# Token mixer of a two-layer network: 64-column chunk matrices, both head pairs in turn, and a scan whose own values are made beforehand

## The chip, the core and the metric

The kernel runs on one core of a Trainium2 chip. The core has a matrix engine (TensorE, PE in the rows; its weight loads are listed apart as PEld), a vector engine (VectorE, DVE), a scalar engine (ScalarE, ACT), GpSimd (POOL), a queue that issues transfers (SyncE, SP) and 16 DMA engines. Each engine works through its own instructions in a fixed order and waits on semaphores for the others. Matmuls read SBUF and write PSUM, which has eight banks of 512 float32 columns for each of 128 partitions. The metric is device time of one execution in microseconds (us).

## The reference

The network is two blocks (feed-forward, token mixer, feed-forward, gated embedding, each closed by a layer norm) and then a second part with attention and experts. Only the token mixer concerns us; it runs twice. Its third of the mixed width called GDN is a gated delta rule in chunks of 64 tokens, for 4 heads of 128:

```python
gcum = jnp.cumsum(g, axis=-1)
decay = jnp.exp(jnp.where(incl, gcum[..., :, None] - gcum[..., None, :], -jnp.inf))
k_beta = k * beta[..., None]
m = jnp.where(strict, jnp.einsum('nbhik,nbhjk->nbhij', k_beta, k) * decay, 0.0)   # 64 x 64 a chunk
t_inv = lax.linalg.triangular_solve(eye + m, jnp.broadcast_to(eye, m.shape), left_side=True, lower=True)
u = jnp.einsum('nbhij,nbhjv->nbhiv', t_inv, v * beta[..., None])
w = jnp.einsum('nbhij,nbhjk->nbhik', t_inv, k_beta * jnp.exp(gcum)[..., None])
qk = jnp.einsum('nbhik,nbhjk->nbhij', q, k) * decay

def step(state, xs):                       # over 4 chunks, one after the other
    u_c, w_c, qk_c, q_c, k_c, gl = xs
    v_new = u_c - jnp.einsum('bhik,bhkv->bhiv', w_c, state)
    o = jnp.einsum('bhik,bhkv->bhiv', q_c, state) + jnp.einsum('bhij,bhjv->bhiv', qk_c, v_new)
    state = state * gl[..., None, None] + jnp.einsum('bhik,bhiv->bhkv', k_c, v_new)
    return state, o
```

The other two thirds are stick-breaking attention (4 heads of 64, 256 tokens, float32) and a gated short convolution. The three results are concatenated and projected.

## The kernel before, in words

All 256 tokens are two tiles of 128 (`NT`). A weight matrix comes from HBM in pieces of 1 MB (`piece`), each split by ScalarE and VectorE into a high and a low part (`split`, lines 303 and 304), and each product with them is three matmuls (`mm3`, and `proj_T` at line 539 for projections that come out transposed, tile `pT`).

`token_mix` (line 935) lays out the work. `gdn_z` and `gdn_ab` project the gate; `gdn_qkv` projects key, query and value of one head pair (two heads) with their convolution; `gdn_gates` and `gdn_rows` make the decay rows. `gdn_prepare` (line 681), called once for each head pair, solves the triangular systems. It puts a tile of 128 tokens, that is two chunks of 64, into one 128 x 128 matrix whose off-diagonal 64 x 64 blocks are zero by the mask. The inverse is built in levels of 4, 16 and 64: helper `mul` (line 707) does four 128 x 128 products for the pair, two in each of two PSUM tiles, and VectorE (`L718`) or ScalarE (`L715`) takes each tile out. Tiles: `U` and `Dm` the masked matrix, `T1`/`T2` the helper product, `X` the inverse, `XT` its transpose, `NT` a product between levels, `wT` the matrix w, `aT` the query-key matrix (it overwrites `g_e`), `kdec` and `qd` decayed key and query, `vb` value times beta.

`gdn_scan` (line 777) goes through four chunks (`t`, `cc`). For each it makes X times values and w times state in one PSUM accumulation (lines 797 and 799), copies it to `vn`, makes the state's increment (line 810), the new state (`L822`, VectorE), and the output (line 831 with the state, line 832 with `vn`). Row and column slices `r` are the chunk's 64 partitions. `stick_breaking` gives four generators, one a head; `weave` advances the scan and at most two heads by turns. `short_conv` comes last.

What sets the order: a scheduler places instructions on each engine by priority, which follows the order of the program text; `later(-1000)` gives a part an earlier priority. Projections (`pT`, `pj`) fill the places between. PSUM tiles come from three pools: `mm_bank` and `ch_bank` with three banks each, `tr_bank` with two. SBUF work tiles come from rings (`s`, `g`, `gc`).

Of the kernel before, what the change touches and what calls it, by code (L numbers as in the profile page):

```python
# [12 lines left out]
ALU = mybir.AluOpType  # L13
AX = mybir.AxisListType
PSUM = bass.MemoryType.PSUM
P = 128

# [34 lines left out]
class Net:  # L52
# [82 lines left out]

    def col(self, n, name, dtype=F32):
        return self.tmp.tile([P, n], dtype, tag=f"col{n}", name=name)

# [12 lines left out]
    def masks(self):  # L151
# [31 lines left out]
        self.m4 = block("m4", self.su, 4)  # L183
        s16 = block("s16", self.su, 16, self.s("s16")[:, :P])
        self.m16 = self.c([P, P], "m16")
        g.tensor_tensor(self.m16, s16, self.m4, ALU.subtract)
        self.m64 = block("m64", self.su, 64)
        g.tensor_tensor(self.m64, self.m64, s16, ALU.subtract)
# [343 lines left out]
    def proj_T(self, src, use):  # L532

        xT = self.xT
        for j, (hi, lo) in enumerate(self.piece(src, KD, 2 * P, by=1)):
            o = self.mm_bank("pT")
# [41 lines left out]
    def gdn_gates(self, i, ab):  # L578
# [42 lines left out]
        rows = [self.gdn_rows(gr, g, beta, gc) for gr in range(2)]  # L621
        return dict(beta=beta, kd=kd, egl=egl, beg=beg, rows=rows)

    def gdn_rows(self, gr, g, beta, gc):
# [8 lines left out]
        eg, e, br = self.g("g_eg"), self.g("g_e"), self.g("g_br")  # L633
        e4 = e.rearrange("p (n w) -> p n w", n=4)
        nc.vector.tensor_tensor(e4, pr.rearrange("p (n w) -> p n w", n=4), self.bl(gc[:, s], P), ALU.subtract)
        nc.vector.tensor_scalar(e, e, 0.0, None, ALU.min)
        self.tact(e, e, AF.Exp)
        nc.vector.tensor_tensor(e4, e4, self.bc(self.mi, 4), ALU.mult)
# [7 lines left out]
        return eg, e, br  # L646
# [15 lines left out]
    def l2n(self, src, out, bias):  # L662
# [4 lines left out]
        pn = self.mm_bank("l2p")  # L667
# [5 lines left out]
    def gdn_qkv(self, i, gr):  # L673
        out = []
        for c0 in (4, 0, 8):
# [5 lines left out]
    def gdn_prepare(self, gr, G, kqv):  # L681
# [4 lines left out]
        eg, E, br = G["rows"][gr]  # L686
        kn, qn, vc = kqv
        n4 = lambda z: z.rearrange("p (n w) -> p n w", n=4)
        self.l2n(kn, kn, 0.0)
        kb, qd = self.g("kb"), self.g("qd")  # L690
        v.tensor_tensor(kb, kn, br, ALU.mult)
        self.l2n(qn, qn, self.c_lns)
        sl = [slice(n * P, n * P + P) for n in range(4)]
        hf = [slice(n * S, n * S + S) for n in range(2)]
        n2 = lambda z: z.rearrange("p (n w) -> p n w", w=P)
        U = self.g("U")
        for j in range(2):
            p = self.ch_bank("pkk")
            for n in (2 * j, 2 * j + 1):
                mm(p[:, sl[n]], kn[:, sl[n]], kb[:, sl[n]], start=True, stop=True)  # L700
            v.tensor_tensor(U[:, hf[j]], p[:, hf[j]], E[:, hf[j]], ALU.mult)
        Dm, T1, L1 = self.g("Dm"), self.g("T1"), self.g("L1")
        for j in range(2):
            v.tensor_tensor(n2(Dm[:, hf[j]]), n2(U[:, hf[j]]), self.bc(self.m4, 2), ALU.mult)
            v.tensor_tensor(n2(T1[:, hf[j]]), self.bc(self.ident, 2), n2(Dm[:, hf[j]]), ALU.subtract)

        def mul(name, l, r, base, o=None):

            o = self.g(name) if o is None else o
            for j in range(2):  # L710
                p = self.ch_bank(name)
                for n in (2 * j, 2 * j + 1):
                    mm(p[:, sl[n]], l[:, sl[n]], r[:, sl[n]], start=True, stop=True)
                if base is None:
                    nc.scalar.activation(o[:, hf[j]], p[:, hf[j]], AF.Copy)  # L715
                else:
                    b = self.bc(self.ident, 2) if base is self.ident else n2(base[:, hf[j]])
                    v.tensor_tensor(n2(o[:, hf[j]]), b, n2(p[:, hf[j]]), ALU.subtract)  # L718
            return o

        DT = self.g("DT")
        for j in range(2):
            p = self.ch_bank("pd")
            for n in (2 * j, 2 * j + 1):
                nc.tensor.transpose(p[:, sl[n]], Dm[:, sl[n]], self.ident)
            nc.scalar.activation(DT[:, hf[j]], p[:, hf[j]], AF.Copy)
        T1 = mul("T2", DT, T1, self.ident, T1)
        v.tensor_tensor(n4(L1), n4(U), self.bc(self.m16, 4), ALU.mult)
        XT = mul("XT", T1, DT, self.ident)
        X = mul("X", DT, T1, self.ident)  # L730
        v.tensor_tensor(n4(U), n4(U), self.bc(self.m64, 4), ALU.mult)
        v.tensor_tensor(qd, qn, eg, ALU.mult)
        aT = E
        for j in range(2):
            p = self.ch_bank("pqk")
            for n in (2 * j, 2 * j + 1):
                mm(p[:, sl[n]], kn[:, sl[n]], qn[:, sl[n]], start=True, stop=True)
            v.tensor_tensor(aT[:, hf[j]], p[:, hf[j]], E[:, hf[j]], ALU.mult)
        for lev, L in enumerate((L1, U)):
            NTm = mul("NT", L, XT, None)  # L740
            T = mul("T1", NTm, X, X)
            if lev == 0:
                cs = slice(gr * 4, gr * 4 + 4)
                col = lambda z: self.bl(z[:, cs], P)
                pk = self.ch_bank("pk")
                for n in range(4):
                    nc.tensor.transpose(pk[:, sl[n]], kn[:, sl[n]], self.ident)
                kg, kdec, vb = self.g("kg"), self.g("kdec"), self.g("vb")
                v.tensor_tensor(n4(kg), n4(pk), col(G["beg"]), ALU.mult)
                v.tensor_tensor(n4(kdec), n4(pk), col(G["kd"]), ALU.mult)  # L750
                pv = self.ch_bank("pv")
                for n in range(4):
                    nc.tensor.transpose(pv[:, sl[n]], vc[:, sl[n]], self.ident)
                v.tensor_tensor(n4(vb), n4(pv), col(G["beta"]), ALU.mult)
# [4 lines left out]
        wT = mul("wT", kg, X, None)  # L759
        return dict(X=X, wT=wT, vb=vb, qd=qd, aT=aT, kdec=kdec)  # L760

# [14 lines left out]

    def gdn_scan(self, G, H, zs, mT):

# [3 lines left out]
        po = [self.tr_bank("gdn_o") for _ in range(NT)]  # L782
        ends = []
        for t in range(NT):
            vn = self.g("vn")
            for cc in range(2):
                r = slice(cc * 64, cc * 64 + 64)
                sl = lambda h: slice((h % 2) * S + t * P, (h % 2) * S + t * P + P)
                sc = lambda h: slice((h % 2) * S + t * P + cc * 64, (h % 2) * S + t * P + cc * 64 + 64)
                last = t == NT - 1 and cc == 1  # L790
                pb = [self.ch_bank("gdn_vS") for _ in range(2)]
                for pr in range(2):
                    A = H[pr]
                    for j in range(2):
                        h = 2 * pr + j
                        hs = slice(j * P, j * P + P)
                        mm(pb[pr][r, hs], A["X"][:, sc(h)], A["vb"][:, sl(h)], start=True, stop=St[pr] is None)
                        if St[pr] is not None:
                            mm(pb[pr][r, hs], A["wT"][:, sc(h)], St[pr][:, hs], start=False, stop=True)
                yield  # L800
                for pr in range(2):
                    nc.vector.tensor_copy(vn[r, pr * S:pr * S + S], pb[pr][r, :S])
                yield
                old = list(St)
                for pr in range(2):
                    if last:
                        continue
                    for j in range(2):
                        h = 2 * pr + j
                        mm(pb[pr][:, S + j * P:S + j * P + P], H[pr]["kdec"][r, sl(h)], vn[r, h * P:h * P + P], start=True, stop=True)  # L810
                yield
                for pr in range(2):
                    if last:
                        continue
                    Sn = self.tmp.tile([P, S], F32, name="gdn_St", bufs=4)
                    if St[pr] is None:
                        nc.vector.tensor_copy(Sn, pb[pr][:, S:])
                    else:
                        for j in range(2):
# [3 lines left out]
                                                           pb[pr][:, S + j * P:S + j * P + P], ALU.mult, ALU.add)  # L823
                    St[pr] = Sn
                yield
                for h in range(GH):
                    A = H[h // 2]
                    hs = slice(h * P, h * P + P)
                    js = slice((h % 2) * P, (h % 2) * P + P)
                    if old[h // 2] is not None:  # L830
                        mm(po[t][r, hs], A["qd"][:, sc(h)], old[h // 2][:, js], start=True, stop=False)
                    mm(po[t][r, hs], A["aT"][r, sc(h)], vn[r, hs], start=old[h // 2] is None, stop=True)
# [3 lines left out]
            ends.append(self.gdn_out(t, po[t], zs[t], mT))  # L836
# [19 lines left out]
    def stick_breaking(self, i, mT):  # L856
# [9 lines left out]

        def usev(t, o):
            nc.scalar.activation(v[:, t * 256:t * 256 + 256], o, AF.Copy)
        self.proj(w[:, 512:768], 256, usev)
# [1109 lines left out]
```

## Time and profile before

| | |
|---|---|
| three runs | median 1696.42 us (1693.31 to 1701.42) |
| the profiled execution | 1690.66 us, span of its instructions 1688.9 us |
| TensorE busy | 1627.1 us, 96% of the span |
| VectorE, ScalarE busy | 1315.7 us (78%), 901.2 us (53%) |
| DMA | 202 GB/s read on average |
| first token mixer | about 203 to 383 us of the span |
| second token mixer | about 816.7 to 987.7 us |

Busy time of TensorE counts a matmul until its result has drained, and matmuls overlap, so an engine that is always busy may still have less to issue. What matters for TensorE is the distance from one start to the next, which the rows of a timeline show.

### The profile page before, as it was taken

What the parts mean: (1) busy time and instruction counts of PE and PEld (TensorE: products, weight loads), DVE (VectorE), ACT (ScalarE), POOL (GpSimd) and SP (SyncE); (2) the same over time, 40 slices, a digit from 0 to 9 for tenths busy, and PEclk for the clock granted to TensorE, in tenths of its full rate; (3) what the DMA queues carried; (4) which work ended last, traced back from release to release, by engine and by line L of the source; (5) the groups of instructions that cost most, each with busy time, mean ns of one, the idle gap of its engine ahead of it and who ended that gap; (6) DMA issues with size and microseconds to landing.
All of it is one profiled execution on the core that took longest, in us unless ns stands there. A gap on an engine that the chain in (4) does not pass through costs nothing.

```text
span 1688.9 us, 23445 instructions
## 1 busy us (share of the span) xinstructions
PE 1627.1 (96%) x8655; PEld 1365.6 (81%) x8655; DVE 1315.7 (78%) x2449; ACT 901.2 (53%) x1601; POOL 21.8 (1%) x80
## 2 busy tenths in 40 slices
PE   8999999999999989999999999999898889999998
PEld 6888898888888868888889888888687678787876
DVE  7669888568669786688886676687868869899896
ACT  6543375355543435444563535544466558676774
POOL 1000000000000000000000000000100000000000
PEclk9999999999999999999999999999989989999999
DMA  8667662145558756567541246576443329899995
GB/s 292 202 213 255 197 178 81 51 150 189 185 200 281 245 165 198 176 251 243 174 132 51 100 150 211 198 263 226 153 142 112 128 100 336 314 340 329 364 337 196
DMA packets 175193, 342.39 MB, mean 203 GB/s; under 512 B 12969, under 2 KB 49890, under 8 KB 175074
## 3 DMA queue, kind: packets, MB, share of 16 engines
q1 hardware_dynamic: 175074, 340.84, 59.2%
q8 instruction: 70, 1.15, 0.3%
q14 instruction: 49, 0.40, 0.1%
HBM read 339.76 MB, written 1.05 MB: 202 GB/s over the span
## 4 chain that ended last, share of the span: by engine, by line
PE 87%; DVE 8%; ACT 3%; DMA 1%; issue 1%; SPq 0%; DVEq 0%; ACTq 0%
PE gu L298 10%; PE gu L299 10%; PE gu L300 10%; PE pT L539 7%; PE y L300 5%; PE y L298 5%; PE y L299 5%; PE moe_h L299 3%; PE moe_h L300 3%; PE moe_h L298 3%; DVE wlo L304 2%; PE moe_y L299 2%; PE moe_y L298 2%; PE moe_y L300 2%; PE pt L319 1%; PE pt L449 1%
## 5 line engine op out<-in xcount | busy, mean ns | idle before, releaser
L304 DVE TENSOR_TENSOR wlo<-wraw,whi 128x512 fp32r<-128x512 f32 (+3 forms) x752 | 605.5, 836 | 172.1 <-ACT whi L303 169.4
L303 ACT ACTIVATE whi<-wraw 128x512 fp32r<-128x512 f32 (+3 forms) x752 | 528.0, 746 | 362.5 <-issue 103.9
L298 PE MATMUL gu<-whi,xTh 128*128 128x512 f32 (+1 forms) x736 | 274.8, 373 | 0.0
L299 PE MATMUL gu<-wlo,xTh 128*128 128x512 f32 (+1 forms) x736 | 274.2, 373 | 0.0
L300 PE MATMUL gu<-whi,xTl 128*128 128x512 f32 (+1 forms) x736 | 273.8, 372 | 0.0
L298 PEld LDWEIGHTS gu<-whi,xTh 128*128 128x128 f32 x736 | 138.5, 188 | 23.2
L300 PEld LDWEIGHTS gu<-whi,xTl 128*128 128x128 f32 x736 | 138.5, 188 | 23.1
L299 PEld LDWEIGHTS gu<-wlo,xTh 128*128 128x128 f32 x736 | 138.6, 188 | 22.8
L539 PE MATMUL pT<-xTl,whi 128*128 128x256 f32 x352 | 101.7, 290 | 0.0
L539 PE MATMUL pT<-xTh,whi 128*128 128x256 f32 x352 | 101.6, 289 | 0.0
L539 PE MATMUL pT<-xTh,wlo 128*128 128x256 f32 x352 | 101.5, 289 | 0.0
L298 PE MATMUL y<-whi,hTh 128*128 128x512 f32 x224 | 87.7, 391 | 0.0
L300 PE MATMUL y<-whi,hTl 128*128 128x512 f32 x224 | 87.6, 391 | 0.0
L299 PE MATMUL y<-wlo,hTh 128*128 128x512 f32 x224 | 87.2, 389 | 0.0
L298 PE MATMUL y<-whi,xTh 128*128 128x512 f32 x192 | 75.9, 395 | 1.7 <-ACT xTh L303 1.7
L299 PE MATMUL y<-wlo,xTh 128*128 128x512 f32 x192 | 74.8, 390 | 0.0
L300 PE MATMUL y<-whi,xTl 128*128 128x512 f32 x192 | 74.3, 391 | 0.0
L1093 DVE SCALAR_TENSOR_TENSOR ada<-ada_w,silu_c,ada 128x512 f32<-128x512 f32 x84 | 62.7, 746 | 12.6 <-DMA ada_w<-in_w_ada_dram 12.1
L539 PEld LDWEIGHTS pT<-xTh,whi 128*128 128x128 f32 x352 | 67.4, 191 | 1.2 <-issue 1.2
L539 PEld LDWEIGHTS pT<-xTl,whi 128*128 128x128 f32 x352 | 67.2, 191 | 1.0 <-issue 1.0
L539 PEld LDWEIGHTS pT<-xTh,wlo 128*128 128x128 f32 x352 | 67.4, 191 | 0.5 <-issue 0.5
L1206 DVE SCALAR_TENSOR_TENSOR bias<-rel_m,rel_delta,bias 128x384 f32<-128x384 bf16 x116 | 63.9, 611 | 0.5
(561 smaller groups left out, 3194.7 us busy)
## 6 DMA issues: line engine op xcount, KB each, us to landing
wraw<-in_ffn_w_in_dram SPq DMA_DIRECT2D x88, 1024.0 KB
wraw<-in_ffn_w_out_dram SPq DMA_DIRECT2D x44, 1024.0 KB
wraw<-in_mix_w_in_dram SPq DMA_DIRECT2D x28, 1024.0 KB
ada_w<-in_w_ada_dram SPq DMA_DIRECT2D x96, 256.0 KB
wraw<-in_w_gate_dram SPq DMA_DIRECT2D x20, 1024.0 KB
wraw<-in_w_up_dram SPq DMA_DIRECT2D x19, 1024.0 KB
wraw<-in_w_down_dram SPq DMA_DIRECT2D x19, 1024.0 KB
wraw<-in_mix_w_out_dram SPq DMA_DIRECT2D x8, 1024.0 KB
```

The source lines that it names most:

```text
L298: mm(out, l[0], r[0], start=start, stop=False)
L299: mm(out, l[0], r[1], start=False, stop=False)
L300: mm(out, l[1], r[0], start=False, stop=stop)
L303: h = self.split_hi = self.nc.scalar.activation(hi, src, AF.Copy).ins
L304: self.mark = self.nc.vector.tensor_tensor(lo, src, hi.bitcast(F32), ALU.subtract).ins
L319: self.nc.tensor.transpose(pt[:, j * P:(j + 1) * P], src[:, (c + j) * P:(c + j + 1) * P], self.ident)
L449: nc.tensor.transpose(pt[:, f * P:f * P + P], h[:, f * P:f * P + P], self.ident)
L539: self.nc.tensor.matmul(o[:, :S], w[:, k], z[:, k], start=k == 0 and n == 0, stop=k == KD - 1 and n == 2)
L1093: z = nc.vector.scalar_tensor_tensor(acc, raw, c, acc, ALU.mult, ALU.add)
L1206: z = nc.vector.scalar_tensor_tensor(b, m, d, b, ALU.mult, ALU.add)
```

## The change

The helper matrices become 64 columns wide: a tile of 128 tokens keeps its two chunks as two 64 x 64 blocks on partitions 0 to 63 and 64 to 127, and drops the zero blocks. `near` tiles hold both halves for one head pair in 256 columns. Every product `mul` is then 8 matmuls of 64 rows, 64 columns and 64 moving columns for a pair instead of 4 of 128, with the two partition halves in turn, into one PSUM tile, and one VectorE or ScalarE instruction takes a pair's product out instead of two. The masks are made in this form by ten more GpSimd copies at the start. The decay rows are also made in this form (line 658, a new product `g_pn`).

`gdn_prepare` is called once, for both head pairs, which alternate in each step. Key and query of both pairs are projected and normed first; the values' projection comes after `stick_breaking` has projected its query and key. X times values no longer stands in the scan: `gdn_values` makes it for all chunks beforehand (line 830), ScalarE copies it, and the scan adds w times state to it. The scan's outputs are made for both chunks of a tile together (lines 889 and 891), and in a bank per tile. `stick_breaking` advances two heads together on two banks that it keeps, and one pair after the other; `short_conv` and its three work tiles get a bank and slots of their own (tile `sc`).

```diff
+CH = (slice(0, 64), slice(64, 128))
+        def near(name, src):
+            m = self.c([P, 64], name)
+            for r in CH:
+                g.tensor_copy(m[r], src[r, r])
+            return m
+        self.n4, self.n16, self.n64 = near("n4", m4), near("n16", m16), near("n64", m64)
...
+        for n in range(4):
+            for r in CH:
+                nc.tensor.matmul(pn[r, n * 64:n * 64 + 64], gb[:, n, r], self.mi[:, r], start=True, stop=True)
...
+        nl = [slice(n * 64, n * 64 + 64) for n in range(4)]
+        both = [(n, c, r) for n in range(4) for c, r in enumerate(CH)]
+        near = lambda name: [(z := self.g(name))[:, :S], z[:, S:]]
         def mul(name, l, r, base, o=None):
-            o = self.g(name) if o is None else o
-            for j in range(2):
-                p = self.ch_bank(name)
-                for n in (2 * j, 2 * j + 1):
-                    mm(p[:, sl[n]], l[:, sl[n]], r[:, sl[n]], start=True, stop=True)
...
-                    v.tensor_tensor(n2(o[:, hf[j]]), b, n2(p[:, hf[j]]), ALU.subtract)
+            o = near(name) if o is None else o
+            for gr in range(2):
+                p = self.ch_bank(name)
+                for n, c, h in both:
+                    mm(p[h, nl[n]], l[gr][h, nl[n]], rr[c][h] if r is self.ident else r[gr][h, nl[n]], start=True, stop=True)
...
+                    v.tensor_tensor(n2(o[gr]), b, n2(p[:, :S]), ALU.subtract)
...
+    def gdn_values(self, H, t):
+        p, u = self.ch_bank("gdn_u"), self.g("vn")
+        for h in range(GH):
+            n = h % 2 * NT + t
+            A = H[h // 2]
+            for r in CH:
+                mm(p[r, h * P:h * P + P], A["X"][r, n * 64:n * 64 + 64], A["vb"][r, n * P:n * P + P], start=True, stop=True)
+        self.nc.scalar.activation(u, p, AF.Copy)
...
-                        mm(pb[pr][r, hs], A["X"][:, sc(h)], A["vb"][:, sl(h)], start=True, stop=St[pr] is None)
+                        mm(pb[h // 2][r, js], H[h // 2]["wT"][:, sc(h, cc)], St[h // 2][:, js], start=True, stop=True)
+                        nc.vector.tensor_tensor(z, pb[pr][r, :S], z, ALU.add)
...
+                for cc, r in enumerate(CH):
+                    if old[cc][0] is not None:
+                        mm(po[r, hs], A["qd"][:, sc(h, cc)], old[cc][h // 2][:, js], start=True, stop=False)
+                for cc, r in enumerate(CH):
+                    mm(po[r, hs], A["aT"][r, nl(h)], vn[r, hs], start=old[cc][0] is None, stop=True)
...
-                H.append(self.gdn_prepare(gr, G, kqv[gr]))
+        with self.later(-1500):
+            H = self.gdn_prepare(G, k, q, vc)
+        self.weave([self.behind(self.gdn_scan(G, H, zs, mT), -1000), heads])
         self.short_conv(i, mT)
```

On TensorE, in the upper level of the solve for one head pair, the kernel before has this (a `T_` number is a tile's; `x2` is a number of matmuls):

```order
L713 MATMUL NT<-XT,U 128x128 x4
L539 MATMUL pT<-xTh,wlo 128x256
L713 MATMUL T_2761<-X,NT 128x128 x2
L713 MATMUL T_2765<-X,NT 128x128 x2
...
L713 MATMUL T_2769<-T_2760,NT 128x128 x2
L713 MATMUL T_2773<-T_2760,NT 128x128 x2
```

The changed kernel has this on TensorE in the same stretch of the first level, for both head pairs:

```order
L743 MATMUL NT<-XT,L_2994 64x64 x16
L743 MATMUL T_3021<-X,NT 64x64 x8
L743 MATMUL T_3031<-X,NT 64x64 x8
L776 MATMUL pqk<-gdn_c 64x64 x16
L743 MATMUL T_3061<-T_3020,NT 64x64 x8
L743 MATMUL T_3071<-T_3020,NT 64x64 x8
L559 MATMUL pT<-xTh,wlo 128x256
```

Two matmuls of 128 for half a pair have become eight of 64 for a whole one, and the step of the other pair stands where the second half stood; the order repeats itself half as often in a mixer.

On VectorE, the stretch that takes these products out reads like this before (`L671`, `L691` and `L701` belong to the norm and the first product of the other pair, `L304` to the split of weights):

```order
L718 TENSOR_TENSOR XT<-XT 128x256 x2
L718 TENSOR_TENSOR X<-X 128x256 x2
L671 TENSOR_TENSOR gdn_c<-gdn_c,l2sq 128x512
L718 TENSOR_TENSOR T_2760<-X,T_2761 128x256
L718 TENSOR_TENSOR T_2760<-X,T_2765 128x256
```

and now like this:

```order
L324 TENSOR_TENSOR wlo<-wraw,whi 128x512
L777 TENSOR_TENSOR g_e<-pqk,g_e 128x256 x2
L748 TENSOR_TENSOR T_3020<-X,T_3061 128x256
L748 TENSOR_TENSOR T_3020<-X,T_3071 128x256
L748 TENSOR_TENSOR XT<-XT 128x256 x2
L748 TENSOR_TENSOR X<-X 128x256 x2
L790 TENSOR_TENSOR kg<-pk,g_beg 128x512
L791 TENSOR_TENSOR kdec<-pk,g_kd 128x512
```

The instructions are as wide as before, but the two of a step now serve two pairs, where before they served the two halves of one.

On TensorE in the scan, the kernel before has this from the increment of one chunk's state to the next chunk's values (`gdn_vS` is both w times state and the increment, `sb_` tiles are attention, `pj` a projection):

```order
L810 MATMUL gdn_vS<-vn,kdec 128x128 x2
L831 MATMUL gdn_o<-gdn_St,qd 64x128
L832 MATMUL gdn_o<-vn,g_e 64x128
...
L797 MATMUL gdn_vS<-vb,X 64x128
L799 MATMUL gdn_vS<-gdn_St,wT 64x128
...
L298 MATMUL pj<-whi,xTh 128x256
L891 MATMUL sb_l<-sb_e,nsl 128x128
```

The changed kernel has this (`gdn_dS` is the increment, `gdn_vS` w times state alone, and `g_eg` now holds the decayed query):

```order
L865 MATMUL gdn_dS<-vn,kdec 128x128 x4
L891 MATMUL gdn_o<-vn,g_e 64x128
L889 MATMUL gdn_o<-gdn_St,g_eg 64x128
L891 MATMUL gdn_o<-vn,g_e 64x128 x2
...
L855 MATMUL gdn_vS<-gdn_St,wT 64x128 x4
L889 MATMUL gdn_o<-gdn_St,g_eg 64x128
L938 MATMUL sb<-sbq,sbk 128x256
L940 MATMUL sb<-sbq,sbk 128x128
```

The X products are gone from the scan, and fewer projections stand between its steps; the two chunks' outputs stand side by side. Outside the two mixers the order of every engine is that of before, except for the GpSimd copies.

## Rows read from the trace of the kernel before

**Rows 1.** The page: busy time of the engines over the span.

```profile
PE 1627.1 (96%) x8655; PEld 1365.6 (81%) x8655; DVE 1315.7 (78%) x2449; ACT 901.2 (53%) x1601; POOL 21.8 (1%) x80
```

**Rows 2.** By stretch: us; busy (count) of PE, PEld, DVE, ACT, POOL; clock, DMA, GB/s.

```profile
262.20:285.10 22.90, 21.55 (x170) 19.56 (x168) 20.18 (x45) 12.92 (x25) 0.00 (x0) 1.00 0.18 59
285.10:309.20 24.10, 24.09 (x201) 23.06 (x199) 17.67 (x39) 6.10 (x16) 0.00 (x0) 1.00 0.13 45
309.20:342.90 33.70, 32.94 (x236) 25.90 (x235) 17.34 (x40) 13.97 (x35) 0.00 (x0) 1.00 0.08 32
```

**Rows 3.** What TensorE waited for within the solve's first stretch, 262.2 to 285.1.

```profile
PE pd L725 <- DVE Dm L704: 0.8, 1, 0.8
PE T L713 <- ACT DT L726: 0.5, 1, 0.5
```

**Rows 4.** Timeline of TensorE in the solve: start, us, instruction, rows*columns, count.

```profile
297.67 0.28 PE L539 MATMUL pT<-xTh,wlo 128*128 128x256 f32 x1
297.79 0.28 PE L539 MATMUL pT<-xTl,whi 128*128 128x256 f32 x1
...
298.15 1.06 PE L713 MATMUL XT<-NT,T 128*128 128x128 f32 x8
299.04 1.06 PE L713 MATMUL X<-T,NT 128*128 128x128 f32 x8
...
301.08 1.16 PE L713 MATMUL T<-X,NT 128*128 128x128 f32 x8
...
302.31 1.15 PE L713 MATMUL T<-T,NT 128*128 128x128 f32 x8
```

**Rows 5.** Timeline of VectorE beside it: the same, and idle time before with its releaser.

```profile
301.83 0.87 DVE L718 TENSOR_TENSOR T<-X,T 128x256 f32<-128x256 f32 x2 [1.27 <-PE T L713]
303.05 0.87 DVE L718 TENSOR_TENSOR T<-X,T 128x256 f32<-128x256 f32 x2 [0.36 <-PE T L713]
```

**Rows 6.** Records in the first mixer, by line and shape: count, busy us, mean ns.

```profile
L832 PE MATMUL gdn_o<-vn,g_e 64*64 64x128 f32 x32 | 6.2, 290 | 0.0
L797 PE MATMUL gdn_vS<-vb,X 128*64 128x128 f32 x32 | 5.8, 277 | 0.0
L831 PE MATMUL gdn_o<-gdn_St,qd 128*64 128x128 f32 x24 | 5.1, 294 | 0.0
L725 PE MATMUL pd<-ident,Dm 128*128 128x128 f32 x8 | 1.6, 287 | 0.8 <-DVE Dm L704 0.8
L304 DVE TENSOR_TENSOR wlo<-wraw,whi 128x512 fp32r<-128x512 f32 x49 | 32.8, 685 | 8.5 <-ACT whi L303 8.3
L303 ACT ACTIVATE whi<-wraw 128x1024 fp32r<-128x1024 f32 x8 | 8.4, 1055 | 4.0 <-PE pT L539 3.9 <-PE pj L300 0.2
```

**Rows 7.** Busy time of line 713 alone, first mixer (TensorE, its weight loads).

```profile
203.00:383.00 180.00, 28.65 (x208) 25.34 (x208) 1.00 0.37 119
```

**Rows 8.** Timeline of TensorE in the scan, shapes by turns or kept.

```profile
334.85 0.38 PE L797 MATMUL gdn_vS<-vb,X 128*64 128x128 f32 x2
335.07 0.38 PE L799 MATMUL gdn_vS<-gdn_St,wT 128*64 128x128 f32 x2
...
338.39 0.43 PE L831 MATMUL gdn_o<-gdn_St,qd 128*64 128x128 f32 x2
338.76 0.43 PE L832 MATMUL gdn_o<-vn,g_e 64*64 64x128 f32 x2
```

**Rows 9.** Timeline of TensorE where two halves of the array are addressed in turn.

```profile
328.30 0.32 PE L903 MATMUL sb_l<-sb_zs,sbv 128*64 128x128 f32 x1
328.41 0.27 PE L904 MATMUL sb_l<-sb_zs,sbv 128*64 128x128 f32 x1
328.46 0.27 PE L903 MATMUL sb_l<-sb_zs,sbv 128*64 128x128 f32 x1
...
328.73 0.38 PE L799 MATMUL gdn_vS<-gdn_St,wT 128*64 128x128 f32 x2
```

**Rows 10.** Timeline of TensorE at the router, the smallest matmuls of the trace.

```profile
1351.51 0.40 PE L1640 MATMUL rt_b<-w_router,modcols 128*1 128x20 f32 x10
```

More of the change, by code (lines that the diff above doesn't have):

```diff
@@ L134, in weave, with behind @@
                     steps = steps[1:]
+    def behind(self, z, n):
+        while True:
+            with self.later(n):
+                end = next(z, self) is self
+            if end:
+                return
+            yield
     def col(self, n, name, dtype=F32):
@@ L530, in sc_tap, with proj_T @@
         return self.taps[:, n:n + 1]
-    def proj_T(self, src, use):
+    def proj_T(self, src, use, bank=None):
         xT = self.xT
         for j, (hi, lo) in enumerate(self.piece(src, KD, 2 * P, by=1)):
-            o = self.mm_bank("pT")
+            o = self.mm_bank("pT") if bank is None else bank[:, j * S:j * S + S]
             for k in range(KD):
@@ L679, in gdn_qkv, with gdn_norm, gdn_prepare @@
         return out
-    def gdn_prepare(self, gr, G, kqv):
+    def gdn_norm(self, G, k, q):
+        v = self.nc.vector
+        for gr in range(2):
+            eg, br = G["rows"][gr]
+            self.l2n(k[gr], k[gr], 0.0)
+            v.tensor_tensor(br, k[gr], br, ALU.mult)
+        for gr in range(2):
+            eg, br = G["rows"][gr]
+            self.l2n(q[gr], q[gr], self.c_lns)
+            v.tensor_tensor(eg, q[gr], eg, ALU.mult)
+    def gdn_prepare(self, G, k, q, vc):
         nc = self.nc
@@ L721, in gdn_prepare @@
[L721 to L738, printed above, removed]
+        n2 = lambda z: z.rearrange("p (n w) -> p n w", w=64)
+        both = [(n, c, r) for n in range(4) for c, r in enumerate(CH)]
+        near = lambda name: [(z := self.g(name))[:, :S], z[:, S:]]
@@ new lines, in gdn_prepare @@
+        U, Dm, T1 = near("U"), near("Dm"), near("T1")
+        for gr in range(2):
+            p = self.ch_bank("pkk")
+            for n, c, r in both:
+                mm(p[r, nl[n]], k[gr][:, cl[n][c]], G["rows"][gr][1][:, cl[n][c]], start=True, stop=True)
+            v.tensor_tensor(U[gr], p[:, :S], E[:, hf[gr]], ALU.mult)
+            v.tensor_tensor(n2(Dm[gr]), n2(U[gr]), self.bc(self.n4, 4), ALU.mult)
+            v.tensor_tensor(n2(T1[gr]), self.bc(self.nid, 4), n2(Dm[gr]), ALU.subtract)
@@ L739, in gdn_prepare @@
+        DT = mul("DT", Dm, self.ident, None)
+        T1 = mul("T2", DT, T1, self.nid, T1)
+        XT = mul("XT", T1, DT, self.nid)
+        X = mul("X", DT, T1, self.nid)
+        L1 = near("L1")
+        for gr in range(2):
+            v.tensor_tensor(n2(L1[gr]), n2(U[gr]), self.bc(self.n16, 4), ALU.mult)
+            v.tensor_tensor(n2(U[gr]), n2(U[gr]), self.bc(self.n64, 4), ALU.mult)
+        H = []
         for lev, L in enumerate((L1, U)):
@@ L742, in gdn_prepare @@
             if lev == 0:
[L743 to L754, printed above, removed]
+                for gr in range(2):
+                    aT = E[:, hf[gr]]
+                    p = self.ch_bank("pqk")
+                    for n, c, r in both:
+                        mm(p[r, nl[n]], k[gr][:, cl[n][c]], q[gr][:, cl[n][c]], start=True, stop=True)
+                    v.tensor_tensor(aT, p[:, :S], aT, ALU.mult)
             T = mul("T2", NTm, T, X, T)
@@ L800, in gdn_scan @@
                 yield
                 for pr in range(2):
[L802 to L810, printed above, removed]
@@ L822, in gdn_scan @@
                             nc.vector.scalar_tensor_tensor(Sn[:, hs], St[pr][:, hs], G["egl"][:, cc, n:n + 1],
-                                                           pb[pr][:, S + j * P:S + j * P + P], ALU.mult, ALU.add)
+                                                           pd[pr][:, hs], ALU.mult, ALU.add)
                     St[pr] = Sn
                 yield
[L826 to L832, printed above, removed]
                 for z in list(ends):
@@ L906, in head @@
             yield
-            self.split(mT[0][r, c], mT[1][r, c], pl[r, :S])
-        return [head(c, hh) for c in range(2) for hh in range(2)]
+            for hh, r in enumerate(CH):
+                self.split(mT[0][r, c], mT[1][r, c], pl[hh][r, :S])
+        bank = [self.mm_bank("sb") for _ in CH]
+        for c in range(2):
+            yield from pair(c, bank)
     def short_conv(self, i, mT):
@@ L943, in token_mix @@
             G = self.gdn_gates(i, ab)
-        kqv.append(self.gdn_qkv(i, 1))
-        H = []
-        for gr in range(2):
-            self.act_set(SILU_SET)
-            for z in kqv[gr]:
-                self.tact(z, z, AF.Silu)
-            self.act_set(LOG_SET)
-            with self.later(-1000):
-                H.append(self.gdn_prepare(gr, G, kqv[gr]))
+        self.act_set(SILU_SET)
+        for z in k + q:
+            self.tact(z, z, AF.Silu)
+        self.act_set(LOG_SET)
+        self.gdn_norm(G, k, q)
         heads = self.stick_breaking(i, mT)
-        with self.later(-1000):
-            self.weave([self.gdn_scan(G, H, zs, mT)] + heads, 3)
+        vc = next(heads)
         self.act_set(SILU_SET)
+        for z in vc:
+            self.tact(z, z, AF.Silu)
+        self.act_set(LOG_SET)
+        next(heads)
+        with self.later(-1500):
+            H = self.gdn_prepare(G, k, q, vc)
+        self.weave([self.behind(self.gdn_scan(G, H, zs, mT), -1000), heads])
         self.short_conv(i, mT)
+        self.act_set(SILU_SET)
         gb = self.ln_params(i, 1)
```

213 lines of the change are left out of this document (123 added, 90 removed).

## The prediction

> **What bounds the kernel now.** I read the page first, then busy time by stretch, the waits, the timelines of the two mixers, and the counts by line. TensorE is busy for 96% of the span [rows 1], so I asked in the mixer whether it issues or waits. In the stretch of the first solve it is busy for 21.55 of 22.90 us, in the second for 24.09 of 24.10, in the scan for 32.94 of 33.70, at a granted clock of 1.00, which is 2.4 GHz [rows 2]. Its waits within the first solve are 0.8 and 0.5 us [rows 3]. So in the mixer the bound is what TensorE has to issue, and a saved issue slot counts as time as long as the next step's input is there. VectorE is the second bound: 20.18 of 22.90 us in the first solve, 17.67 of 24.10 in the second [rows 2].
>
> The currency is the distance between starts. A projection's matmul comes every 0.12 us, eight records of a 128 x 128 product take 0.89 us, that is 0.111 us each [rows 4], and in plain float32 each product matmul leaves two records (the order has four where the timeline has eight); a transpose leaves one. When the shape stays the same, a record with 128 moving columns on 64 array columns also takes 0.11 us (a pair 0.22); where two shapes take turns, a pair takes 0.37 us [rows 8]. So a change of shape costs about 0.15 us; I use 0.14.
>
> **The change part by part, for one mixer.** I count records before and after, and price them.
>
> The price that the trace doesn't have is that of a 64 x 64 record with 64 moving columns. Alone it should take half of 0.109, 0.055 us, since the stream is half as long. But the change addresses the two halves of the array in turn, and rows show what turns do: from 328.41 to 328.73 us six records of two column halves start in 0.32 us, 0.053 each instead of 0.109 [rows 9]. Two halves at once thus halve the price, to 0.028 us for the new records. Starts can be as near as that: ten records at the router begin 0.025 us apart [rows 10]. The bounds are 0.028 and 0.055 us; I take 0.028, because the nearest rows are those of the turns, and keep the other end as a rival.
>
> - Solve: 13 products. Before, 208 records of line 713 [rows 7], of which 16 are `wT`, so 192 x 0.112 = 21.5 us, and 8 transposes of line 725 [rows 6], 0.9 us. After, 13 x 16 matmuls x 2 = 416 records x 0.028 = 11.6 us. Change -10.8 (alone: 22.9, so +0.5).
> - The two products of key with key and query: 32 records of 0.112 become 64, 3.6 to 1.8 us: -1.8 (alone -0.1). `wT`: 16 become 32, 1.8 to 0.9: -0.9 (alone 0). The new `g_pn`: 32 records: +0.9 (alone +1.8).
> - X times values: 32 records [rows 6] of 0.109 become 32 with 128 moving columns, on two halves in turn: 3.5 to 1.8 us, -1.7 (alone 0).
> - Scan outputs: 32 + 24 records [rows 6], 6.1 us at 0.109 without the changes of shape. After, chunks stand side by side, and all but 8 records have a partner in the other half: 48 x 0.055 + 8 x 0.109 = 3.5 us, -2.6 (alone 0).
> - w times state and the state's increment keep their records, and each addresses one half only: 0.
> - Changes of shape: going down TensorE's order in the mixer, the rows or columns used change 49 times before and 79 times after. 30 x 0.14 = +4.2 us. Projections left between small products cost this twice.
>
> The sum in issue is -10.8 - 1.8 - 0.9 + 0.9 - 1.7 - 2.6 + 4.2 = -12.7 us.
>
> Then the waits. A step of the solve now has TensorE issue two pairs (2 x 16 x 0.028 = 0.9 us, with two changes of shape 1.2), and VectorE take out two products, 0.87 us for two [rows 5], as many as it took for one pair. Before, a step's start-to-start was 1.23 us for one pair, with VectorE waiting 0.36 us in it [rows 4, 5]. So the chain of a step, 1.2 us, serves two pairs and fits under TensorE's own issue, barely. Over the whole solve TensorE has 512 small records, eight transposes and 42 projections, 14.3 + 0.9 + 5.0 us, with 26 changes of shape (3.6) 23.8 us. VectorE has in the same stretch 32 operations of 0.435, six of 128x512 near 0.685 and six splits of 0.685 [rows 5, 6]: 22.1 us. Before these were two stretches of 47 us together, with 75 projections and other fillers in them. Two engines that are nearly full and depend on each other lose something: the splits stand in VectorE's queue ahead of products in the first level, and TensorE waits there. I add 1.5 us. At the scan's start ScalarE copies X times values, behind a weight split of 1.06 us [rows 6], and TensorE has only three projections to issue in the meantime: 1 us. In attention the second pair now begins after the first has freed its banks: 1.5 us. Together 4.0 us of new waits, bounds 0 and 9; against them the 1.3 us of rows 3 go, since both pairs now alternate there. Net +2.7.
>
> A mixer thus becomes 10.0 us shorter, two 20 us. Nothing else is on the path: the ten GpSimd copies stand at the start on an engine that is busy 21.8 us in all [rows 1], and their masks are first used some 250 us later; if that cover were gone they would cost a few us once. The order outside the mixers doesn't move. One transfer on SP's queue (a piece of `ada_w`) now stands behind the layer norm's rows, and is used in the next feed-forward stage.
>
> The profiled execution took 1690.66 us, so it would become 1670.7. It lies 5.8 us under the median of the runs shown; on that basis I forecast 1696.4 - 20 = 1676 us.
>
> **Rivals.** *The halves don't run at once.* The evidence for turns in rows 9 is of two heads that write two different banks; the new products write one bank from both halves. If the array keeps such a pair apart, every record costs its price alone: +0.5 - 0.1 + 1.8 + 4.2 = +6.4 us a mixer. The solve is then bound by TensorE (a step 2.1 us against a chain of 1.2), so the waits vanish, -1.3. That is +5.1 a mixer and 1696.4 + 10 = 1706 us, on the other side. It decides from a record price of about 0.045 us up: between 0.028 and 0.055 the issue sum moves by 19.1 us, and some 11 of these use up the gain and the waits it left. The Trainium skill speaks for this rival: "TensorEngine Tiling (Array Packing)", Restrictions and Gotchas, says that different row tiles cannot access the same PSUM bank simultaneously. No row here has two row halves in one bank. By that rule the time would be this rival's 1706; I give it less than the forecast because the two halves here also write different partitions.
>
> *The waits take most of it.* The price is right, but the solve becomes a chain of VectorE's queue and the scan, robbed of its projections, runs at its own latency. VectorE's 22.1 us with one queue, in which splits wait for ScalarE (8.5 us of such idle time in the mixer [rows 6]), speaks for it; that TensorE's issue in the stretch is no shorter than VectorE's speaks against. With the upper bound of 9 us of waits instead of 4 the gain is 12.7 + 1.3 - 9 = 5 us a mixer: 1686 us.
>
> *More than forecast.* Changes of shape hidden behind weight loads and no new waits: -12.7 - 4.2 + 2 - 1.3, about -16 a mixer, 1664 us. The pairs at 0.37 in rows 8 speak against it, since nothing is waited for there.
>
> **How the numbers follow.** Forecast 0.53, waits 0.22, halves apart 0.15, more 0.10. About 0.5% (8.5 us) is what a measurement of this kernel can tell from no change, so faster means under 1688. The forecast and the better case fall under it, and somewhat more than half of the waits: 0.75 less some tenth for sizes I mis-set, 0.71. Within: the rest of the waits and a part of the case with the halves apart (its price may lie between), 0.17. Slower 0.12. The range reaches from the better case to nearly the slow one, 1660 to 1704; the forecast's own is 1668 to 1685.
>
> **What would show it.** Records of the new products (line 743) starting about 0.03 us apart, sixteen in 0.45 us, show the price right; 0.055 shows the first rival. The solve of both pairs should be one stretch of about 26 us from its first product to `wT`, in place of two of 23 and 24. The scan should show TensorE's waits for VectorE of some tenths, not of whole us. I am wrong if the projections themselves come late, because the weights' splits or transfers can't keep up with a shorter mixer: then waits for ScalarE or DMA would stand in front of `pT` and `sc`. I am also wrong if the stages outside the mixers move by more than 2 us.

## The result and the profile after

| | median | runs |
|---|---|---|
| before | 1698.41 us | 4, 1693.31 to 1701.42 |
| changed | 1673.16 us | 4, 1671.07 to 1677.51 |
| ratio | 0.9856 | 95% interval 0.9831 to 0.9882 |

The forecast was 1676 us. The profiled execution after took 1672.71 us, and the span of its instructions is 1670.9. TensorE is still the engine that is busy ([rows 1] has the kernel before; a record is one instruction in the trace):

```profile
PE 1614.5 (97%) x9247; PEld 1346.8 (81%) x9247; DVE 1289.5 (77%) x2389; ACT 899.0 (54%) x1593; POOL 24.4 (1%) x90
```

I take a mixer from the first start of its leading projection (`pj`) to the first start of the next feed-forward stage. The two mixers after, as stretches (us; busy time and count of PE, PEld, DVE, ACT, POOL; clock, DMA share, GB/s):

```profile
202.97:374.05 171.08, 168.84 (x1588) 147.07 (x1588) 125.02 (x282) 94.46 (x194) 0.00 (x0) 1.00 0.39 126
794.10:966.70 172.60, 170.35 (x1588) 148.16 (x1588) 125.04 (x282) 94.45 (x194) 0.00 (x0) 0.99 0.39 125
```

The same two in the kernel before:

```profile
203.53:387.37 183.84, 179.59 (x1292) 159.80 (x1292) 138.26 (x312) 95.77 (x198) 0.00 (x0) 1.00 0.37 117
808.20:992.14 183.94, 179.63 (x1292) 159.82 (x1292) 138.26 (x312) 95.67 (x198) 0.00 (x0) 1.00 0.37 117
```

The first mixer is 12.8 us shorter, the second 11.3. In the second the granted clock fell during its leading projection, which took 12.9 in place of 11.4 us; without that it would be 12.8 too. TensorE's idle time in a mixer (length less busy) went from 4.25 to 2.24 us, so of the 12.8 us 10.7 are issue and 2.0 are waits.

The solve, from the first product of keys to `wT`, is one stretch of 24.1 us (some 26 were forecast), and VectorE lies beside TensorE in it; before, it took 43.6 us, from 262.2 to 305.8, within the first two stretches of [rows 2]:

```profile
259.49:283.58 24.09, 24.07 (x531) 21.57 (x531) 20.37 (x46) 8.17 (x16) 0.00 (x0) 1.00 0.16 47
```

Two of its products in the timeline of TensorE (start, us, instruction, array rows*columns, count), against [rows 4]:

```profile
265.24 0.28 PE L559 MATMUL pT<-xTh,wlo 128*128 128x256 f32 x1
265.45 1.15 PE L743 MATMUL XT<-DT,T 64*64 64x64 f32 x32
266.43 1.10 PE L743 MATMUL X<-T,DT 64*64 64x64 f32 x32
```

From the start of XT to that of X, 32 records take 0.98 us, 0.031 each with the change of shape in it. Starts lie alternately 0.006 and 0.052 us apart: two halves start together, and a pair takes 0.058.

This is all that TensorE waited for in the first mixer. The waits of [rows 3] are gone, and none stands in the solve or at the scan's start; the last line is the only one in attention:

```profile
PE pj L318 <- ACT xTh L323: 1.1, 1, 1.1
PE pt L339 <- DVE x L415: 0.6, 2, 0.3
PE sb L972 <- DVE sb_zs L967: 0.3, 1, 0.3
```

Outside the mixers one stage moved far: the second attention's output projection (`wo`), from its first start to its last, took 60.4 us in place of 51.9. Its middle, after:

```profile
1304.30:1327.00 22.70, 17.98 (x56) 13.04 (x56) 14.79 (x43) 8.50 (x32) 0.23 (x1) 0.62 0.15 47
```

And before, the same 56 records:

```profile
1330.93:1346.12 15.19, 11.50 (x56) 8.27 (x56) 12.97 (x36) 7.28 (x28) 0.23 (x1) 1.00 0.19 70
```

The granted clock, between its levels of 2.4 and 1.2 GHz, was 1.00 before and 0.62 on average after. TensorE is busy longer over the same work because each matmul takes longer: those of `wo` start every 0.43 us where the clock is at 0.50, and every 0.23 us where it is at 1.00. Of the 7.5 us between the two rows 1.6 are one longer wait at the start (1.99 us in place of 0.37).

### The profile page after: what moved, and what is told of

Read it like the earlier page. It is cut to its first block, busy times and chain, and to the rows that moved or that the text cites. A ratio compares the mean times of both kernels' runs of the same rounds, so it can differ in the third digit from the quotient of the medians.

```text
span 1670.9 us, 24511 instructions
## 1 busy us (share of the span) xinstructions
PE 1614.5 (97%) x9247; PEld 1346.8 (81%) x9247; DVE 1289.5 (77%) x2389; ACT 899.0 (54%) x1593; POOL 24.4 (1%) x90
## 4 chain that ended last, share of the span: by engine, by line
PE 86%; DVE 7%; ACT 3%; DMA 2%; issue 1%; SPq 0%; DVEq 0%; ACTq 0%
PE gu L318 10%; PE gu L319 9%; PE gu L320 9%; PE pT L559 5%; PE y L320 5%; PE y L318 5%; PE y L319 5%; PE moe_h L319 3%; PE moe_h L320 3%; PE moe_h L318 3%; PE sc L559 2%; PE moe_y L319 2%; PE moe_y L318 2%; PE moe_y L320 2%; PE pt L339 2%; PE pj L318 2%
## 5 line engine op out<-in xcount | busy, mean ns | idle before, releaser
L559 PE MATMUL pT<-xTh,whi 128*128 128x256 f32 x256 | 74.6, 291 | 0.0
L559 PE MATMUL pT<-xTh,wlo 128*128 128x256 f32 x256 | 74.4, 291 | 0.0
L559 PE MATMUL pT<-xTl,whi 128*128 128x256 f32 x256 | 73.4, 288 | 0.0
L109 ACT ACTIVATE ffn_h<-gu 128x512 f32<-128x512 f32 (+1 forms) x48 | 27.0, 563 | 56.3 <-PE gu L320 56.3
L323 ACT ACTIVATE xTh<-pt 128x512 fp32r<-128x512 f32 (+1 forms) x72 | 35.6, 500 | 39.7 <-PE pt L339 34.2
L319 PE MATMUL moe_h<-wlo,moe_xh 128*128 128x512 f32 x128 | 50.8, 397 | 1.7 <-DVE wlo L324 1.7
```

The costliest lines, as they stand in the source:

```text
L109: ins = self.nc.scalar.activation(*args, **kw).ins
L319: mm(out, l[0], r[1], start=False, stop=False)
L323: h = self.split_hi = self.nc.scalar.activation(hi, src, AF.Copy).ins
```

## The experiments

Theory A is the prediction's: TensorE's issue bounds the mixer. Rival B: the gain comes from the turns of the two pairs, which hide VectorE. Mixers below are corrected for a fall of the clock in their leading projection, as above. Ratios are to before.

**Halves apart** (`x1`).

```diff
-        both = [(n, c, r) for n in range(4) for c, r in enumerate(CH)]
+        both = [(n, c, r) for c, r in enumerate(CH) for n in range(4)]
```

> The changed kernel, but in every chunk product (line 743, the key products and wT) all four matmuls of one half of the array are issued before the four of the other half. Theory A, TensorE's issue bounds the mixer and half of the gain is two halves at once: of 16 records 14 now start 0.052 us apart and 2 at 0.007, 0.74 us in place of 0.47; with 480 such records a mixer gets 8 us longer, 16 in all, so about 1689 us. Rival B, the gain is that both pairs take turns and VectorE has half as much to take out: VectorE, busy 20.5 of the solve's 24.2 us, covers most of it, under 4 us a mixer, at most 1681 us. For wT, whose pairs of row halves write all 128 partitions and take 0.111 us: if they already run one after the other, nothing changes (0.055 each); if they overlap, 0.11 each.

Measured 1680.4 us, ratio 0.9913 [0.9891, 0.9934]. Both mixers take 176.6 us, +5.5, all of it in the solve, where TensorE is always busy and VectorE's work is the same:

```profile
259.45:289.08 29.63, 29.63 (x532) 27.23 (x531) 20.59 (x46) 8.27 (x16) 0.00 (x0) 1.00 0.13 38
```

The mixer's +5.5 us lies between the two (8 and under 4); the time alone would fit B. A record without a partner takes 0.058 us, so the price of one half alone is as A has it. But grouping did not keep the halves apart. All of `XT` is issued before `X`, and yet records of `X` in one half start before the last ones of `XT` in the other:

```profile
267.72 0.27 PE L743 MATMUL X<-T,DT 64*64 64x64 f32 x1
267.77 0.22 PE L743 MATMUL XT<-DT,T 64*64 64x64 f32 x1
267.83 0.22 PE L743 MATMUL X<-T,DT 64*64 64x64 f32 x1
267.83 0.22 PE L743 MATMUL XT<-DT,T 64*64 64x64 f32 x1
```

So the mean distance rose to 0.041, not 0.046. Against B: VectorE covered nothing. `wT` took 2.46 us from its first start to its last, as in the changed kernel. Its records without a partner take 0.111 to 0.112 us each, as much as a pair takes in the changed kernel, so the pairs do overlap, which I had held open.

**Pair after pair, 64 columns** (`x2`).

```diff
-            H = self.gdn_prepare(G, k, q, vc)
+            H = [self.gdn_prepare(G, k, q, vc, [gr], near) for gr in range(2)]
...
```

> The changed kernel with its 64-column products, but the first head pair is solved to its end before the second begins. Theory A (issue bounds): TensorE has projections to put between the steps, more in the first solve than in the second; where they last nothing is lost, in the second solve some 2 us of waits and more changes of shape, so 2 to 4 us a mixer, 1677 to 1681 us. Rival B (the turns are the gain): each step again waits for VectorE, 0.3 to 0.4 us in each of 13 products and two pairs, 8 to 10 us a mixer, 1690 us or more.

Measured 1678.4 us, ratio 0.9890 [0.9871, 0.9909]; the mixers 174.2, +3.1, as A expected. TensorE waits for nothing over both solves:

```profile
261.27:312.78 51.51, 51.51 (x737) 45.71 (x737) 35.96 (x74) 25.18 (x48) 0.00 (x0) 1.00 0.29 94
```

More projections stand between the steps, and the shape changes 109 times in a mixer instead of 85. Comparing records beside a change with the same records elsewhere, the changes cost some 15 us instead of 12, about the 3.1 us (such a comparison is good to about half a microsecond). Of `wT`, the 16 records of a head pair now stand together, in overlapping pairs, and take 0.84 us from first to last start, 1.7 in all in place of 2.46:

```profile
281.70 1.11 PE L796 MATMUL wT<-X,kg 64*128 64x64 f32 x16
```

**Wide by turns** (`x3`): the kernel before, with `gdn_prepare` as a generator per pair and both woven. For this, both pairs' projections and norms come first, and some work tiles are shared.

```diff
...
+            self.weave([self.gdn_prepare(gr, G, kqv[gr], H) for gr in range(2)])
```

> The kernel before, with its 128-column products and its scan, but both head pairs take turns in each step of the solve. Theory A: the records of the solve stay 2 x 23 us, only the waits of 1.3 us a mixer can go; 1692 to 1698 us, no change that can be measured. Rival B: the larger part of the gain comes from the turns, 1675 to 1685 us.

Measured 1704.7 us, ratio 1.0044 [1.0025, 1.0062]: slower than either expected. The solve of both pairs has no wait left, as A has it (before 42.2 us busy in 43.6):

```profile
273.13:312.40 39.27, 39.27 (x343) 38.94 (x342) 32.23 (x74) 9.84 (x24) 0.00 (x0) 1.00 0.10 34
```

But the norms of both pairs now stand ahead of the solve, and TensorE waits there for the last convolution, which I had not costed:

```profile
PE l2p L668 <- DVE gdn_c L657: 3.3, 1, 3.3
PE l2p L668 <- ACT l2sq L108: 0.6, 1, 0.6
```

Right behind this wait the granted clock was at its lower level for 6.8 us, in both mixers; the first:

```profile
265.30:272.10 6.80, 5.92 (x14) 3.35 (x15) 2.96 (x6) 6.53 (x10) 0.00 (x0) 0.50 0.46 158
```

By TensorE's busy time there that costs about 3 us, an estimate. With the 3.9 us of waits it outweighs the 4.3 us by which the solve is shorter, and the first mixer took 189.0 us in place of 183.8 (about 1.5 of it a fall in the leading projection). So this form of the turns does not pay; that the turns at this width could pay with the values projected late was not tried.

**Outputs by kind** (`x4`).

```diff
+            for kind in range(2):
+                for h in range(GH):
...
+                        if kind == 0 and old[cc][0] is not None:
...
+                        if kind == 1:
```

> The changed kernel, but the scan's output products of one block are issued by kind: first those with the state for all four heads, then those with the values, so 1 change of shape in place of 7 in each of the two blocks. By the 0.10 us that a change of shape takes in the changed kernel's trace beyond a record's own time: 12 x 0.1 = 1.2 us a mixer shorter (171.1 to 169.9 us), 2.4 in all, 1671 us. Rival: changes of shape are hidden behind the stationary loads, no difference.

Measured 1670.3 us, ratio 0.9855 [0.9819, 0.9890], which by time alone cannot be told from the changed kernel. In the trace the stretch from the first output to the next stage is 0.88 us shorter in the first mixer and 0.86 in the second, less than the 1.2 expected but not nothing. The output products now run on as one group:

```profile
321.17 1.09 PE L892 MATMUL gdn_o<-vn,g_e 64*64 64x128 f32 x16
322.19 0.39 PE L559 MATMUL sc<-xTh,whi 128*128 128x256 f32 x1
```

where the changed kernel has

```profile
312.27 0.43 PE L891 MATMUL gdn_o<-vn,g_e 64*64 64x128 f32 x2
312.63 0.43 PE L889 MATMUL gdn_o<-gdn_St,g_eg 128*64 128x128 f32 x2
313.00 0.44 PE L891 MATMUL gdn_o<-vn,g_e 64*64 64x128 f32 x4
```

**Values in the scan** (`x5`).

```diff
-        vns = [self.gdn_values(H, t) for t in range(NT)]
...
+                    mm(pb[h // 2][r, js], A["X"][r, n * 64:n * 64 + 64], A["vb"][r, n * P:n * P + P], start=True, stop=St[0] is None)
+                    if St[0] is not None:
+                        mm(pb[h // 2][r, js], A["wT"][:, sc(h, cc)], St[h // 2][:, js], start=False, stop=True)
...
```

> The changed kernel, but X times values is made again inside the scan, one half of the array at a time, into the bank to which w times state is added. Theory A (issue bounds): its 32 records take 0.109 us alone in place of 0.055 in turns, +1.6 us a mixer, and the two shapes now alternate, some 24 changes at 0.07 to 0.1 us, +1.7 to 2.4: 3.3 to 4 us a mixer, 1680 to 1682 us. Rival B: the scan is a chain of VectorE's steps, and the products made beforehand only fill gaps: less than 1 us a mixer, 1673 to 1675 us.

Measured 1684.8 us, ratio 0.9926 [0.9891, 0.9960]; the mixers take 177.9 and 178.2 us, +6.9: A's direction, but nearly twice its size.

```profile
321.61 0.43 PE L854 MATMUL gdn_vS<-vb,X 64*64 64x128 f32 x2
321.97 0.43 PE L856 MATMUL gdn_vS<-gdn_St,wT 128*64 128x128 f32 x2
322.33 0.43 PE L854 MATMUL gdn_vS<-vb,X 64*64 64x128 f32 x2
```

The two shapes take turns at 0.36 us a pair, as in [rows 8]. From start to start the X records went from 2.04 to 5.42 us, w times state from 3.35 to 4.35, and most of the rest is products of attention heads (+1.9), of which more run without a partner in the other half. With chunk matrices it thus pays to make X times values beforehand: in the kernel before both products had one shape.

**`wT` moving 128 columns** (`x6`).

```diff
-                mm(p[c][:, nl[n]], H[gr]["kg"][r, sl[n]], X[gr][r, nl[n]], start=True, stop=True)
+                m = min(n, 2) * 64
+                mm(p[c][:, n * 64 + m:n * 64 + m + 128], H[gr]["kg"][r, sl[n]], X[gr][r, m:m + 128], start=True, stop=True)
...
```

> The changed kernel, but the 32 records of wT move 128 columns in place of 64 (the second half goes to columns that nobody reads). Theory A: a record with 128 stationary columns takes 0.111 us whatever it moves up to 128 columns, so a pair in the two row halves still starts every 0.111 us and the stretch of wT stays 2.46 us. Rival B: wT's 0.111 us per pair are two records of 64 moving columns one after the other, 0.055 each; then 128 columns take 0.22 a pair and wT 4.2 us.

Measured by one run, 1672.4 us. Twice the stream costs 0.1 us in all; the changed kernel has

```profile
283.58 2.74 PE L797 MATMUL wT<-X,kg 64*128 64x64 f32 x32
```

and this one

```profile
283.51 2.84 PE L798 MATMUL wT<-X,kg 64*128 64x128 f32 x32
```

A holds: a record over 128 stationary columns takes 0.111 us, alone or together with its partner, whether 64 or 128 columns move.

**More take-outs** (`x7`, and `x8` with `base is not o` as the condition). A take-out is the VectorE instruction that moves a product out of PSUM.

```diff
+                    for _ in range(1 + (name in ("T2",))):
+                        v.tensor_tensor(n2(o[gr]), b, n2(p[:, :S]), ALU.subtract)
```

> The changed kernel, with 6 of the solve's products a mixer taken out of PSUM by VectorE twice, with the same result: 6 x 0.435 = 2.6 us more on VectorE, 23.1 us in a solve of 24.1 (first product of keys to wT). Theory A (TensorE's issue bounds, VectorE lies beside it): the solve becomes at most 0.5 us longer. Rival B (each step is a chain through VectorE, which the turns only just cover): it becomes some 2 us longer.

> As before, with 14 products a mixer taken out twice: 14 x 0.435 = 6.1 us more, so VectorE's 26.6 us exceed TensorE's 24.1. Theory A: now VectorE is the bound of the stretch and TensorE waits: 26.6 us and a little more, +2.5 to 4 us. Rival B: as each step is a chain, all of it shows, +6 us, 30 us.

One run each, 1672.9 and 1669.4 us. The solve and the rest of the first mixer, with 6 more:

```profile
261.80:289.45 27.65, 27.63 (x558) 24.86 (x557) 23.37 (x53) 9.36 (x20) 0.00 (x0) 1.00 0.25 79
289.45:376.80 87.35, 86.82 (x630) 74.17 (x627) 58.44 (x126) 48.01 (x102) 0.00 (x0) 1.00 0.29 100
```

With 14 more:

```profile
259.45:291.77 32.32, 32.30 (x591) 29.11 (x590) 28.28 (x67) 12.32 (x26) 0.00 (x0) 1.00 0.21 67
291.77:375.04 83.27, 82.74 (x597) 70.16 (x594) 55.31 (x120) 45.13 (x96) 0.00 (x0) 1.00 0.30 105
```

The solve grew by 3.6 and 8.2 us, more than A and even B expected, and yet TensorE never waits in it: it took in 27 and 60 more records, nearly all of them projections that stood behind the solve, and what follows is as much shorter. The first mixer as a whole grew by 0.5 and 1.0 us. Its shape changes 88 and 92 times in place of 85, which at 0.14 us each is 0.4 and 1.0. The chain is tight, as B has it, and costs no wait while projections are left, as A has it.

**The clock** (`y1`, the kernel before again; `y2`, `x4` with fillers).

```diff
+            with self.later(200):
+                for _ in range(3):
+                    mm(pt, self.ident, qT[t], start=True, stop=True)
```

> The kernel before, unchanged, profiled once more. In the changed kernel's profile the output projection of the second attention stage (wo) takes 60.4 us in place of 51.9, at a granted clock of 0.5 for some 15 us. Theory A: this has nothing to do with the change; the profiled execution of before was one in which the clock held there, and another one falls too: wo in 56 to 60 us, 1694 to 1700 us in all. Rival B: the change moves the fall there; then wo takes 52 us again and the time is about 1691.

`y1` took 1702.6 us, above A's 1694 to 1700, `wo` 60.8, and the clock fell in the middle:

```profile
1335.40:1356.90 21.50, 18.64 (x60) 13.39 (x60) 12.27 (x32) 6.29 (x24) 0.23 (x1) 0.60 0.14 49
```

So the change is not needed for the fall; an execution of before has it too. Ahead of it TensorE waits, and the first of these waits differs between executions. In the changed kernel, in the profile of before, in `x1` and in `x8`:

```profile
1306.36 0.59 PE L1618 MATMUL pt<-ident,diff_p 128*128 128x128 f32 x2 [1.99 <-DVE diff_p L1613]
1331.37 0.59 PE L1544 MATMUL pt<-ident,diff_p 128*128 128x128 f32 x2 [0.37 <-DVE diff_p L1539]
1311.87 0.59 PE L1618 MATMUL pt<-ident,diff_p 128*128 128x128 f32 x2 [0.36 <-DVE diff_p L1613]
1309.66 0.59 PE L1619 MATMUL pt<-ident,diff_p 128*128 128x128 f32 x2 [1.75 <-DVE diff_p L1614]
```

Its length does not decide. Behind 0.37 us the clock held, behind 0.36 it was at 0.50 for 17.1 us, and behind 1.75 for only 3.4 us.

> The kernel with the outputs by kind, and nine matmuls of 512 columns whose result nobody reads (they write a transposition's bank before it) in the gaps of the second attention stage, where TensorE waits 2.0, 0.9 and 0.8 us for the softmax and the granted clock then falls to 0.5. Theory A: the clock falls because of these gaps; with them filled it holds and wo's stretch takes 52 to 55 us in place of 57.3, though the fillers add up to 2 us: 1664 to 1668 us. Rival B: it falls all the same, and the fillers stand in the path: 1670 to 1674 us.

`y2` took 1665.7 us (1662.4 to 1673.3), ratio 0.9816 [0.9791, 0.9842], the lowest median of the kernels with several runs; its interval overlaps those of the changed kernel and of `x4`. In the profile `wo` took 54.4 us, and the clock held with a filler where the wait was:

```profile
1311.84 2.74 PE L1619 MATMUL pt<-diff_qT,ident 128*128 128x512 f32 x6
```

and the stretch after it:

```profile
1314.00:1332.00 18.00, 15.78 (x69) 9.59 (x68) 12.79 (x34) 6.80 (x26) 0.23 (x1) 1.00 0.16 59
```

That is one profile, and the slowest of the six executions. Without fillers the clock fell only briefly there in the profiles of before and of `x8` (`wo` 51.9 and 53.8), and for long in the other nine (57.0 to 60.8). One of these is `x4`, where the first wait was 0.33 us, so the fall does not need the wait of 2.0 us. That the fillers keep the clock up is thus possible, not shown, and what makes it fall stays open.

## Why the prediction was right, and where not

- **The price of a record held.** 0.028 us was forecast, 0.029 came (0.058 a pair, as much as a record alone takes in `x1`), and so the first rival is out: both halves write one bank and run at once. The Trainium skill, "TensorEngine Tiling (Array Packing)", Restrictions and Gotchas, says that different row tiles cannot access one PSUM bank at the same time; where the row tiles also write different partitions, as here, the trace does not agree.
- **Changes of shape held.** 30 more at 0.14, +4.2 us, were forecast; the trace has 85 in place of 55 (I had counted 79 and 49), which cost some 12 in place of 8 us, about +4. So the third rival, changes of shape that are hidden and no new waits, has its second half right and its first wrong; the +2 in its sum comes from no row.
- **`wT` failed**: not -0.9 but +0.7. I priced it by the columns that move; `x6` shows that 128 stationary columns set it, so a pair takes 0.111 us, which makes 1.8 us, no change. And it came to 2.5 us, because most records of the second head pair have no partner: the pool has three banks and a head pair takes two, so three matmuls of one half are issued before ScalarE has emptied a bank for the other, and from 284.52 to 286.05 records start 0.10 us apart on average. `x2` has no such wait, and takes 1.7. "TensorE: Matmul & The Clock Gate", LDWEIGHTS, in the Trainium skill says that a weight load takes its time by its columns, whatever its rows; the trace agrees. Its loads of 128 columns take 187 and 191 ns over 64 and 128 rows, those of 64 columns 135 over either:

```profile
L797 PEld LDWEIGHTS wT<-X,kg 64*128 64x128 f32 x32 | 2.6, 187 | 0.1
L559 PEld LDWEIGHTS sc<-xTh,wlo 128*128 128x128 f32 x48 | 9.2, 191 | 0.1
L743 PEld LDWEIGHTS X<-T,NT 64*64 64x64 f32 x64 | 2.0, 135 | 0.1
L855 PEld LDWEIGHTS gdn_vS<-gdn_St,wT 128*64 128x64 f32 x24 | 2.4, 135 | 1.1 <-DVE gdn_St L875 0.4 <-issue 0.2
```

The 1.6 us of `wT` and the record price (416 x 0.001 us) are, to some tenths, the 2.0 us by which issue fell short of -12.7.

- **The step that failed most is "together 4.0 us of new waits".** Of the three one came, in attention, with 0.3 us for 1.5, and the old ones went, the 1.3 us of [rows 3] and 1.1 more: -2.0 us in place of +2.7. TensorE's work in the solve was summed rightly (23.8 us, measured 24.1); the added 1.5 us supposed that TensorE must wait where VectorE is late. `x7` and `x8` show that the order draws on projections when the chain is late: 6.1 us more work on VectorE made the mixer 1.0 us longer. The second rival, waits that take the gain, falls with it.
- **X times values** was forecast at -1.7 (measured 2.04 us for 3.63, -1.6). What undoing it costs, 6.9 us, the prediction didn't see.
- **The sum**: -12.8 a mixer in place of -10.0, from two errors of opposite sign, 2.0 less in issue and 4.7 less in waits. That the time lies within 3 us of the forecast is in part luck: the errors offset each other, and the forecast started from 1696.4 us, the runs beside the result from 1698.4.
- **"Stages outside the mixers" moved by more than 2 us**, which I had named as a sign of error. `y1` shows that the change does not account for it: the profiled execution of before was one in which the clock held. Between the two profiles the mixers gave 24.1 us and all other stages took 6.1 back, to the 18.0 between the spans; `wo` alone took 8.5. On the medians the gain is 25.2 us, which the two mixers' 25.6 account for.

## What to carry to other kernels

Where TensorE's issue bounds a stretch of plain float32 products, count records, price each by the larger of its stationary and moving columns, halve it where the neighbour lies in the other half of the array, and add some 0.14 us for each change of shape; the last two decide how loops are nested. Check whether the partner's PSUM bank is free, or the pair is broken up, as in `wT`. A chain through a second engine costs little while the order has independent work to put into it, so look for that work before adding waits to a forecast. Before explaining a stage that the change doesn't touch, look at the granted clock there, in more than one profile.

## What was not expected of the hardware

Halves of the array run at once even when four matmuls of one half are issued before the other's (`x1`): the mean start distance was 0.041 us, where 0.058 is a record alone and 0.029 a record in turns, and a record in one half started before earlier ones in the other. The clock in one and the same stretch held in some executions and fell in others, with nearly the same waits ahead of it (before and `x1`), and moved a profile by about 8 us, a third of the whole effect measured here.
